# Keeping the gated results of four heads in SBUF and accumulating two projections in the seven-product stage's PSUM banks

## Chip, cores, metric

The kernel runs on 1 core of one Trainium2 chip. The metric is the device time of one launch in microseconds (us); the median of several runs counts.

## What is computed

A small transformer trunk of two layers over 512 frames, with 16 learned tokens in front (L = 528 positions, width 2048), batch 1, float32. Layer A is gated differential attention with 8 heads, layer B gated sliding-window attention with 32 query heads and 4 shared key/value heads. Cut to what matters here:

```
h = rms_norm(x, norm_g)
q, k, v, gate = split(h @ w_in, 4)              # layer A, w_in is 2048 x 8192
o = diff_attention(rope(q), rope(k), v, lam)    # 8 heads, head 7 last
o = rms_norm(o, subln_g) * (1 - lambda_init)
x = x + (o * silu(gate)) @ w_out                # layer A's output projection
k_sh, v_sh = split(rms_norm(x, kv_norm) @ w_kv) # the kv projection
...                                             # layer B, its projections, a final norm
```

## The kernel before

All data lie transposed, features on the 128 partitions and the 528 positions along the free dimension. Each product is made in three passes of a split arithmetic: an operand is cut into a high part (ScalarE copies it rounded, L96 or L739) and a low part (VectorE subtracts, L98, L100 or L740), and high x high, high x low, low x high are accumulated in PSUM. So each weight tile of 128 x 1024 costs one ScalarE and one VectorE instruction of about 1.1 us each before TensorE can use it; these are issued under `tc.high_priority()` (`wunit`, `form`).

Layer A's input projection (w_in) is worked in 32 pairs of 128-row tiles, `PAIRS[0]` to `PAIRS[31]`. The first three are multiplied plainly (`plain`), the other 29 by a scheme with seven products in place of eight (`product`, L361, in the order 1, 5, 2, 6, 3, 4, 7), each of 24 matmuls with 264 columns. The products accumulate in the PSUM pool psP, in the bank tiles B (two buffers), C and D (one each); `BANK` says which product uses which. ScalarE or VectorE empties each bank after its product. Pairs 0 to 23 give q, k and v of the 8 heads, which go to DRAM (`qkv_dram`); pairs 24 to 31 give the gates of heads 0 to 7. A head's attention (`heads_attend`) runs in small steps between the matmuls of later pairs; the result of head h goes to `o_dram[h]`, that of head 7 last, during pair 27.

`finish_gate` works up a gate: it has the head's two 128 x 528 result rows loaded (`gate_in`, L714, on GpSimd's DMA queue) into buffers of the pool ld, which has two; forms the silu in three steps (L725, L727, L728); multiplies by the loaded row on GpSimd (L729); and writes the product to `og_dram` (L731). `og_load` (L742, GpSimd's queue) reads such rows back into the five rows of po5, and `og_in` (L746) splits them into high and low parts for the output projection. The rows of head 7 alone are split from the ld buffer. In the last pairs these steps are spread as the loop at L792 says: rows 0 to 3 are loaded in pair 28 and split in pair 29, the others loaded from pair 30 on and split in pair 31. The high and low parts lie in quads, places of 128 x 2112 words handed out by `Quads`; the forms of product i give theirs back (`Q.free(*ft[i])`) after the last use.

Behind pair 31 the pools of layer A are closed and a new PSUM pool psA with two buffers of two banks is opened (L824). `proj` (L135) multiplies one 128-row output tile: two weight halves, 96 matmuls of 264 columns, both column halves in one accumulator. The output projection has 16 such tiles, each emptied by one VectorE instruction over 528 columns (L871); the kv projection has four (L906 to L913). The output projection needs the first rows' parts at its start and those of the last four rows only in the last quarter of its depth. Then new pools serve layer B.

At the start, `norm_a` computes the norm of x (`rstd`) between the plain pairs, then transposes it to a column `rcol` (L266 to L274). The two results of a plain pair are emptied by ScalarE (L424) into e0x or e0y and into e1, which is one buffer; `finish_qk` scales them and writes them to `qkv_dram` (L480, GpSimd's queue), after which the buffer is free.

Instructions are put in order per engine by a planner that goes by priority and its own estimate of durations; every engine and every DMA queue then works through its list in that order.

Of the kernel before, what the change touches and what calls it, by code (L numbers as in the profile page):

```python
# [43 lines left out]
def trunk(tc, xT, w, vecs, sinks, rope, ident_in, out):  # L44
# [11 lines left out]
    psP = pa.enter_context(tc.tile_pool(name="psP", bufs=1, space=bass.MemoryType.PSUM))  # L56
    steps = deque()
# [77 lines left out]
    def proj(m, hi, lo, cols):  # L135
        acc = psA.tile([128, len(cols), 512], F32, tag="acc", name="acc")
        for half in range(2):
            whi, wlo = wunit(m, half)
            for part in (((whi, hi), (whi, lo)), ((wlo, hi),)):
                for k8 in range(8):  # L140
                    kt = half * 8 + k8
                    ws = slice(k8 * 128, k8 * 128 + 128)
                    for a, b in part:
                        for s, (c0, n) in enumerate(cols):
                            pe.matmul(  # L145
                                acc[:, s, 0:n], lhsT=a[:, ws], rhs=b[kt // 4][:, kt % 4, c0 : c0 + n],
                                start=(kt == 0 and a is whi and b is hi), stop=(kt == KT - 1 and a is wlo),
                            )
                    if kt % 4 == (1 if len(part) == 2 else 3):
                        tick(0.25)  # L150
        return acc
# [109 lines left out]
    def norm_a():  # L261
# [3 lines left out]
        tables(0, 1.0, 128, etmp("rr", "ropec"), ld.tile([128, L], F32, tag="ld", name="ropes"))  # L265
        t = psT.tile([128, 512], F32, tag="T", name="Tr")  # L266
# [130 lines left out]
    def plain(p, between):  # L397

        o = {}
        for t, half in ((0, 0), (1, 0), (0, 1), (1, 1)) if p.m == 0 else ((0, 0), (0, 1), (1, 0), (1, 1)):  # L400
# [17 lines left out]
            if t == 0:  # L418
                p.results()
            else:  # L420
                between()
                p.e[1] = etmp("e1", "e1")
# [291 lines left out]
    def gate_in(p, j, i):  # L714
        p.o.append(ld.tile([128, L], F32, tag="ld", name="ldo"))
        pl.dma_start(p.o[i], o_dram[j][i])

    def finish_gate(p, j, i):
# [10 lines left out]
        pl.tensor_tensor(out=o, in0=z, in1=o, op=ALU.mult)  # L729
        if j < 7:  # L730
            pl.dma_start(og_dram[j][i], o)  # L731
        else:
            split_og(14 + i, o)

    ogh, ogl, ogt = [], [], []

    def split_og(m, src):
        a, b = ogh[m // 4][:, m % 4, :], ogl[m // 4][:, m % 4, :]
# [3 lines left out]
    def og_load(*ms):  # L742
        for m in ms:
            pl.dma_start(po5[:, m % 5, :], og_dram[m // 2][m % 2])

    def og_in(q4):  # L746
# [4 lines left out]
        for m in range(4 * q4, min(4 * q4 + 4, 14)):  # L751
            split_og(m, po5[:, m % 5, :])
# [21 lines left out]
    for j in range(PLAIN):  # L774
# [7 lines left out]
        else:  # L782
            finish(j, 0)
            finish(j, 1)
    for _ in building:
# [6 lines left out]
    for j in range(PLAIN, 32):  # L792
        p, q = PAIRS[j], PAIRS[j + 1] if j < 31 else None
        for i in ORDER:
# [8 lines left out]
            elif i == 6 and j == 28:  # L803
                og_load(0, 1, 2, 3)
            elif i == 6 and j == 29:
                og_in(0)
            elif i == 6 and j == 30:
                og_load(4, 5, 6, 7, 8)
            if q:
                q.load(*{6: ("a",), 5: ("s1",), 7: ("s3",), 3: ("b",), 4: ("d",)}.get(i, ()))  # L810
            else:
                Q.free(*ft[i])
                if i == 1:
                    og_in(1)
                    og_load(9, 10, 11, 12)
                elif i == 5:
                    og_in(2)
                    og_load(13)
                elif i == 2:
                    og_in(3)  # L820
    drain()
    pA.close()
    pa.close()
    psA = psum("psA", 2)  # L824
# [38 lines left out]
    for m in range(KT):  # L863
# [6 lines left out]
        acc = proj(T_OUT_A + m, ogh, ogl, FULL)[:, :, 0:HALF]  # L870
        dve.tensor_tensor(out=two(xr), in0=acc, in1=two(xr), op=ALU.add)  # L871
# [22 lines left out]
    for i in range(4):  # L894
        acc = proj(T_KV + i, kh, kl, FULL)[:, :, 0:HALF]
# [9 lines left out]
        if i < 2:  # L905
            dve.tensor_tensor(out=two(t), in0=acc, in1=two(CR), op=ALU.mult)  # L906
            r = tmp("kr")
            dve.stream_shuffle(out=two(r), in_=acc, mask=swap)
# [3 lines left out]
        else:  # L912
            dve.tensor_tensor(out=two(t), in0=acc, in1=two(rstd), op=ALU.mult)  # L913
            for a, b, c in PIECES:
                act.activation(vx[i - 2][:, a:b], t[:, c : c + b - a], AF.Copy)
    X.free(*ktags)
    ps.close()
# [321 lines left out]
```

## Time and profile before

| | us |
|---|---|
| median of 3 runs (lowest to highest) | 1716.14 (1713.49 to 1717.56) |
| the profiled execution | 1715.63 |
| its span in the trace | 1713.9 |
| TensorE busy (PE) | 96% of the span |
| VectorE (DVE) | 66% |
| ScalarE (ACT) | 50% |
| GpSimd (POOL) | 12% |

In the rows below, times count from the start of the span. PE is a matmul, PEld a weight load, SP the engine that issues most loads; L12 is line 12 of the kernel. A name as `po<-og_dram` is output from input. "[7.68 <-DMA og_dram<-ldo]" says that the engine sat idle for 7.68 us before the instruction, until that DMA had landed. In a chain of waits each piece released the next. PEclk is TensorE's granted clock as a share of full speed.

### The profile page before, as it was taken

To read this page: it belongs to the slowest core of one execution; us is meant where nothing else is said; L and a number is where in the kernel's file an instruction comes from. 1 tells how busy PE (TensorE), PEld (TensorE's weight loads), DVE (VectorE), ACT (ScalarE), POOL (GpSimd) and SP (SyncE) were. 2 spreads that over 40 slices of the span, in tenths; PEclk is the share of its full clock that TensorE was granted. 3 is DMA by queue.
4 is the path that set the end of the run, shared out by engine and by line. 5 is a ranking of instruction groups with operands and counts; after the bars stand their busy time and mean duration, and the time that the engine had idled before them with its cause. 6 is when DMAs were issued, how large, how long until landed. Compare 5 with 4: busy or idle time off the path is not lost.

```text
span 1713.9 us, 28699 instructions
## 1 busy us (share of the span) xinstructions
PE 1651.7 (96%) x11383; PEld 1533.0 (89%) x11383; DVE 1130.0 (66%) x1710; ACT 862.3 (50%) x1628; POOL 212.2 (12%) x246
## 2 busy tenths in 40 slices
PE   8899999999999999889899999999999999999996
PEld 8899999999999999889899999888878888888886
DVE  7877869687687878668433347567766776762234
ACT  9556656566665656544323234254545554543331
POOL 0011111111111113333101110000000000000111
PEclk9999999999999999989899999999999999999998
DMA  8366767676677676677444454222212122233332
GB/s 270 125 180 187 202 168 209 188 212 180 182 220 188 202 213 183 213 197 224 152 137 140 134 152 157 99 83 78 73 63 74 62 81 68 74 117 123 123 117 98
DMA packets 83493, 254.81 MB, mean 149 GB/s; under 512 B 10400, under 2 KB 14624, under 8 KB 83360
## 3 DMA queue, kind: packets, MB, share of 16 engines
q1 hardware_dynamic: 47616, 161.25, 28.2%
q0 software_dynamic: 16992, 59.62, 15.1%
q10 hardware_dynamic: 18752, 32.12, 6.0%
q8 instruction: 89, 1.46, 0.3%
q14 instruction: 44, 0.36, 0.1%
HBM read 223.34 MB, written 29.61 MB: 148 GB/s over the span
## 4 chain that ended last, share of the span: by engine, by line
PE 79%; DVE 7%; issue 5%; DMA 4%; ACT 3%; POOL 2%; DVEq 0%; ACTq 0%; POOLq 0%; SPq 0%
PE acc L145 42%; PE B L355 9%; PE C L355 7%; PE D L355 7%; DVE wlo L98 2%; PE TB L200 1%; PE poB L1032 1%; PE acct L1151 1%; PE B L409 1%; PE po L634 1%; DMA qkv_dram<-e 1%; PE SB L984 1%; PE SB L983 1%; DMA po<-og_dram 1%; PE S L516 1%
## 5 line engine op out<-in xcount | busy, mean ns | idle before, releaser
L98 DVE TENSOR_TENSOR wlo<-raw,whi 128x1024 fp32r<-128x1024 f32 x140 | 171.9, 1228 | 240.5 <-PE acc L145 192.8
L96 ACT ACTIVATE whi<-raw 128x1024 fp32r<-128x1024 f32 x140 | 148.2, 1060 | 219.2 <-PE acc L145 191.3
L145 PE MATMUL acc<-hh,whi 128*128 128x512 f32 x512 | 202.9, 396 | 0.0
L145 PE MATMUL acc<-hl,whi 128*128 128x512 f32 x512 | 201.2, 393 | 0.0
L145 PE MATMUL acc<-hh,wlo 128*128 128x512 f32 x512 | 129.5, 393 | 0.0
L145 PEld LDWEIGHTS acc<-hh,whi 128*128 128x128 f32 x512 | 96.5, 189 | 21.2
L145 PEld LDWEIGHTS acc<-hh,wlo 128*128 128x128 f32 x512 | 95.9, 188 | 21.7
L145 PEld LDWEIGHTS acc<-hl,whi 128*128 128x128 f32 x512 | 96.6, 189 | 20.5
L98 DVE TENSOR_TENSOR wlo<-rs,whi 128x1024 fp32r<-128x1024 f32 x58 | 73.1, 1261 | 29.0 <-ACT whi L96 10.4
L96 ACT ACTIVATE whi<-ra 128x1024 fp32r<-128x1024 f32 x58 | 61.3, 1058 | 59.1 <-PE B L355 24.8
L248 POOL TENSOR_TENSOR ss<-ss,sq 128x528 f32<-128x528 f32 (+1 forms) x26 | 35.0, 1348 | 451.5 <-ACT sq L247 451.5
L96 ACT ACTIVATE whi<-rs 128x1024 fp32r<-128x1024 f32 x58 | 61.2, 1055 | 58.8 <-DMA qkv_dram<-e 20.8
L995 ACT ACTIVATE p<-SB,nm 128x208 f32<-128x208 f32 (+2 forms) x128 | 51.2, 411 | 68.3 <-DVE es L992 61.0
L96 ACT ACTIVATE whi<-rb 128x1024 fp32r<-128x1024 f32 x58 | 61.3, 1057 | 47.6 <-DVE rb L336 13.9
L327 POOL DMA_DIRECT2D rs<-in_w x58 | 51.8, 893 | 251.9 <-DMA rs<-in_w 87.3
L98 DVE TENSOR_TENSOR wlo<-rb,whi 128x1024 fp32r<-128x1024 f32 x58 | 72.4, 1249 | 14.8 <-PE D L355 7.1
L355 PE MATMUL B<-f7h,whi 128*128 128x264 f32 x232 | 60.3, 293 | 6.2 <-ACT e L380 6.2
L355 PE MATMUL D<-f4h,whi 128*128 128x264 f32 x232 | 60.0, 292 | 5.7 <-DVE e L370 3.2
L934 POOL TENSOR_TENSOR qr<-qr,SR 128x512 f32<-128x512 f32 x16 | 22.2, 1387 | 333.6 <-DVE qr L933 266.3
L355 PE MATMUL C<-f5h,whi 128*128 128x264 f32 x232 | 60.1, 292 | 0.0
L355 PE MATMUL C<-f5l,whi 128*128 128x264 f32 x232 | 59.6, 290 | 0.0
L355 PE MATMUL D<-f4l,whi 128*128 128x264 f32 x232 | 59.4, 289 | 0.0
(476 smaller groups left out, 5096.4 us busy)
## 6 DMA issues: line engine op xcount, KB each, us to landing
raw<-in_w SPq DMA_DIRECT2D x148, 512.0 KB, 3.3
rs<-in_w SPq DMA_DIRECT2D x58, 512.0 KB, 3.9
rs<-in_w POOLq DMA_DIRECT2D x58, 512.0 KB, 6.0
rd<-in_w SPq DMA_DIRECT2D x29, 512.0 KB, 4.3
ra<-in_w SPq DMA_DIRECT2D x29, 512.0 KB, 4.6
rb<-in_w SPq DMA_DIRECT2D x29, 512.0 KB, 4.9
qkv_dram<-e POOLq DMA_DIRECT2D x48, 264.0 KB, 4.5
hr<-h_dram ACTq DMA_DIRECT2D x32, 256.0 KB, 3.3
```

The costliest lines, as they stand in the source:

```text
L96: act.activation(hi, raw, AF.Copy, scale=sign)
L98: dve.tensor_tensor(out=lo, in0=raw, in1=f(hi), op=ALU.subtract)
L145: pe.matmul(acc[:, s, 0:n], lhsT=a[:, ws], rhs=b[kt // 4][:, kt % 4, c0 : c0 + n], start=(kt == 0 and a is whi and b is hi), stop=(kt == K ...
L200: pe.transpose(o, i, ident[0 : i.shape[0], 0 : i.shape[0]])
L248: self.engine.tensor_tensor(out=self.acc[i], in0=self.acc[i], in1=t, op=ALU.add)
L327: pl.dma_start(t, w[self.m + 1, 1 if n == "s1" else 0], accum_op=ALU.add)
L355: pe.matmul(o, lhsT=a[:, ws], rhs=b[:, k, :], start=(first and k == 0 and b is fh[i] and a is hi), stop=(last and k == 7 and a is lo), ski ...
L409: pe.matmul(o[t][s], lhsT=a[:, ws], rhs=b[:, k8, :], start=(half == 0 and k8 == 0 and a is x[0] and b is fh[i]), stop=(half == 1 and k8 == ...
L516: pe.matmul(o, lhsT=qh[:, m, qs], rhs=qh[:, 2 + m, ks], start=True, stop=False)
L634: pe.matmul(pov[:, dt, c0:256], lhsT=v_, rhs=w_[:, j, c0:256], start=(j == 0 and k == 0), stop=False)
L934: pl.tensor_tensor(out=r, in0=r, in1=SR[:, META:], op=ALU.mult)
L995: act.activation(p[:, rt, 0:W], Sv[:, rt, :], AF.Exp, bias=nm[:, rt : rt + 1], accum_out=s[:, rt : rt + 1])
```

## The change

Six things are edited.

- The accumulators of the output and kv projections are no longer tiles of a pool psA, but pairs of the bank tiles of psP, by turns (C, D) and (B, B); psP is closed behind the kv projection. Each half of 264 columns is emptied by an instruction of its own.
- For heads 4 to 7, `gate_in` loads the attention result into a place of its own in SBUF (`ograw`), three quads taken after pair 27 and po5; the gated product stays there and is split from there. For heads 0 to 3 it goes to DRAM as before, and all eight rows are read back in pair 29.
- The product with the gate is made on VectorE in place of GpSimd.
- All four groups of rows are split in pair 31, after its products 1, 5, 2 and 6; the split places are those products' freed quads.
- In plain pair 1, the second result goes to an ld buffer in place of e1.
- The transposes that give `rcol` are moved from `norm_a` behind the plain pairs (`rstd_column`).

```diff
     def proj(m, hi, lo, cols):
-        acc = psA.tile([128, len(cols), 512], F32, tag="acc", name="acc")
+        if psA is None:
+            acc = [bank(t) for t in ("CD", "BB")[turns[0] % 2]]
+            turns[0] += 1
+        else:
+            acc = psA.tile([128, len(cols), 512], F32, tag="acc", name="acc")
...
-                                acc[:, s, 0:n], lhsT=a[:, ws], rhs=b[kt // 4][:, kt % 4, c0 : c0 + n],
+                                acc[s] if psA is None else acc[:, s, 0:n], lhsT=a[:, ws], rhs=b[kt // 4][:, kt % 4, c0 : c0 + n],
...
         tables(0, 1.0, 128, etmp("rr", "ropec"), ld.tile([128, L], F32, tag="ld", name="ropes"))
+
+    def rstd_column():
+
         t = psT.tile([128, 512], F32, tag="T", name="Tr")
...
-                p.e[1] = etmp("e1", "e1")
+                p.e[1] = ld.tile([128, L], F32, tag="ld", name="e1") if p.m == 2 else etmp("e1", "e1")
...
     def gate_in(p, j, i):
-        p.o.append(ld.tile([128, L], F32, tag="ld", name="ldo"))
+        p.o.append(ld.tile([128, L], F32, tag="ld", name="ldo") if j < 4 else ograw[j // 2][:, 2 * (j % 2) + i, :])
         pl.dma_start(p.o[i], o_dram[j][i])
...
-        pl.tensor_tensor(out=o, in0=z, in1=o, op=ALU.mult)
-        if j < 7:
+        dve.tensor_tensor(out=o, in0=z, in1=o, op=ALU.mult)
+        if j < 4:
             pl.dma_start(og_dram[j][i], o)
-        else:
-            split_og(14 + i, o)
+        elif j == 7:
+            split_og(14 + i)
...
-    def og_load(*ms):
-        for m in ms:
-            pl.dma_start(po5[:, m % 5, :], og_dram[m // 2][m % 2])
+    def og_places():
+
+        ograw[0] = po5
+        for q4 in range(1, 4):
+            ograw[q4], t = Q.get([128, 4, L], F32, f"ograw{q4}")
+            ogrt.append(t)
+
+    def og_load():
+        for m in range(8):
+            pl.dma_start(ograw[m // 4][:, m % 4, :], og_dram[m // 2][m % 2])
...
+    rstd_column()
     for _ in building:
...
             if i == 7 and j == 27:
                 drain()
-            elif i == 6 and j == 28:
-                og_load(0, 1, 2, 3)
+                og_places()
             elif i == 6 and j == 29:
-                og_in(0)
-            elif i == 6 and j == 30:
-                og_load(4, 5, 6, 7, 8)
+                og_load()
...
                 Q.free(*ft[i])
-                if i == 1:
-                    og_in(1)
-                    og_load(9, 10, 11, 12)
-                elif i == 5:
-                    og_in(2)
-                    og_load(13)
-                elif i == 2:
-                    og_in(3)
+                if i in (1, 5, 2, 6):
+                    og_in((1, 5, 2, 6).index(i))
+    Q.free(*ogrt)
     drain()
     pA.close()
-    pa.close()
-    psA = psum("psA", 2)
+    psA = None
...
-        acc = proj(T_OUT_A + m, ogh, ogl, FULL)[:, :, 0:HALF]
-        dve.tensor_tensor(out=two(xr), in0=acc, in1=two(xr), op=ALU.add)
+        acc = proj(T_OUT_A + m, ogh, ogl, FULL)
+        for c, a in zip(T, acc):
+            dve.tensor_tensor(out=xr[:, c], in0=a, in1=xr[:, c], op=ALU.add)
...
-            dve.tensor_tensor(out=two(t), in0=acc, in1=two(CR), op=ALU.mult)
             r = tmp("kr")
-            dve.stream_shuffle(out=two(r), in_=acc, mask=swap)
+            for c, o in zip(T, acc):
+                dve.tensor_tensor(out=t[:, c], in0=o, in1=CR[:, c], op=ALU.mult)
+                dve.stream_shuffle(out=r[:, c], in_=o, mask=swap)
...
     X.free(*ktags)
+    pa.close()
     ps.close()
```

## Rows read from the trace of the kernel before

**Rows 1.** The page's first part: busy time, share of the span, instructions.
```profile
PE 1651.7 (96%) x11383; PEld 1533.0 (89%) x11383; DVE 1130.0 (66%) x1710; ACT 862.3 (50%) x1628; POOL 212.2 (12%) x246
```
**Rows 2.** What PE waited for: us in total, times, longest (whole span).
```profile
PE B L355 <- ACT e L380: 6.2, 1, 6.2
PE B L355 <- DVE wlo L100: 5.8, 4, 3.2
PE acc L145 <- DVE e L388: 5.7, 1, 5.7
PE B L409 <- ACT e L424: 5.6, 1, 5.6
...
PE D L355 <- DVE e L370: 3.2, 1, 3.2
```
**Rows 3.** Windows: pairs 27 to 31, two projection tiles; length, busy (instructions), PEclk, DMA.
```profile
698.50:722.50 24.00, 20.59 (x167) 20.20 (x166) 19.42 (x20) 11.60 (x16) 7.73 (x11) 1.00 0.76 227
722.50:754.70 32.20, 22.81 (x162) 22.39 (x161) 17.04 (x19) 12.13 (x18) 12.00 (x15) 0.87 0.66 198
754.70:774.70 20.00, 20.00 (x159) 20.00 (x158) 16.90 (x17) 9.83 (x15) 7.69 (x9) 0.95 0.76 215
774.70:795.20 20.50, 20.50 (x170) 20.50 (x169) 17.04 (x17) 9.28 (x13) 6.23 (x7) 1.00 0.75 204
795.20:830.70 35.50, 26.01 (x193) 25.43 (x191) 26.99 (x34) 16.48 (x24) 11.42 (x14) 0.87 0.67 205
830.70:844.50 13.80, 13.80 (x97) 13.80 (x98) 3.23 (x4) 3.41 (x4) 1.32 (x1) 0.84 0.32 113
844.50:856.20 11.70, 11.70 (x98) 11.70 (x98) 3.84 (x4) 3.40 (x4) 0.00 (x0) 1.00 0.43 137
```
**Rows 4.** Chain of waits in pair 28: start, us, what.
```profile
741.08 8.73 DMA po<-og_dram
...
750.39 1.04 ACT whi L96
...
751.76 8.28 PE B L355 x48
```
**Rows 5.** Timeline of POOL in pair 28: start, us, instruction, idle before.
```profile
749.67 0.54 POOL L716 DMA_DIRECT2D ldo<-o_dram  x1 [7.68 <-DMA og_dram<-ldo]
...
757.27 2.10 POOL L729 TENSOR_TENSOR ldo<-e,ldo 128x528 f32<-128x528 f32 x1
```
**Rows 6.** Timeline of PE: the stop in pair 2, the first projection matmul.
```profile
75.98 0.59 PE L409 MATMUL B<-f1h,whi 128*128 128x264 f32 x1 [5.57 <-ACT e L424]
...
830.69 0.78 PE L145 MATMUL acc<-og0h,whi 128*128 128x264 f32 x2 [5.75 <-DVE e L388]
```
**Rows 7.** Timeline of ACT near 76 us.
```profile
75.53 0.39 ACT L424 ACTIVATE e<-B 128x264 f32<-128x264 f32 x1 [4.62 <-DMA qkv_dram<-e]
...
79.33 0.39 ACT L424 ACTIVATE e<-C 128x264 f32<-128x264 f32 x1 [3.13 <-DMA qkv_dram<-e]
```
**Rows 8.** Window behind the stop in pair 2, columns as in rows 3.
```profile
76.00:82.00 6.00, 6.00 (x31) 6.00 (x32) 0.81 (x2) 1.02 (x4) 1.09 (x3) 0.60 0.91 314
```
**Rows 9.** Timeline of DVE: pair 28, and the first projection tile's eviction.
```profile
756.34 0.71 DVE L728 SCALAR_TENSOR_TENSOR e<-th,e 128x528 f32<-128x528 f32 x1 [0.26 <-ACT th L727]
...
758.10 2.35 DVE L98 TENSOR_TENSOR wlo<-rs,whi 128x1024 fp32r<-128x1024 f32 x1
...
845.83 0.70 DVE L871 TENSOR_TENSOR xr<-acc,xr 128x528 f32<-128x528 f32 x1
```
**Rows 10.** DVE groups by line, 795 to 835 us: busy us, mean ns, idle before.
```profile
L740 DVE TENSOR_TENSOR og2l<-po,og2h 128x528 fp32r<-128x528 f32 x4 | 2.8, 705 | 4.7 <-ACT og2h L739 4.7
...
L98 DVE TENSOR_TENSOR wlo<-rs,whi 128x1024 fp32r<-128x1024 f32 x2 | 2.4, 1219 | 0.0
...
L388 DVE TENSOR_TENSOR e<-B,e 128x264 f32<-128x264 f32 x2 | 0.8, 425 | 0.0
```
**Rows 11.** Timeline of DVE near 68 us.
```profile
68.01 0.71 DVE L189 SCALAR_TENSOR_TENSOR rstd<-va,rstd 128x528 f32<-128x528 f32 x1
```

More of the change, by code (lines that the diff above doesn't have):

```diff
@@ L56, in trunk @@
     psP = pa.enter_context(tc.tile_pool(name="psP", bufs=1, space=bass.MemoryType.PSUM))
+    turns = [0]
     steps = deque()
@@ L728, in finish_gate, with split_og @@
         dve.scalar_tensor_tensor(out=z, in0=th, scalar=1.0, in1=z, op0=ALU.add, op1=ALU.mult)
-        pl.tensor_tensor(out=o, in0=z, in1=o, op=ALU.mult)
-        if j < 7:
+        dve.tensor_tensor(out=o, in0=z, in1=o, op=ALU.mult)
+        if j < 4:
             pl.dma_start(og_dram[j][i], o)
-        else:
-            split_og(14 + i, o)
+        elif j == 7:
+            split_og(14 + i)
     ogh, ogl, ogt = [], [], []
-    def split_og(m, src):
-        a, b = ogh[m // 4][:, m % 4, :], ogl[m // 4][:, m % 4, :]
+    ograw, ogrt = {}, []
+    def split_og(m):
+        a, b, src = ogh[m // 4][:, m % 4, :], ogl[m // 4][:, m % 4, :], ograw[m // 4][:, m % 4, :]
         act.activation(a, src, AF.Copy)
         dve.tensor_tensor(out=b, in0=src, in1=f(a), op=ALU.subtract)
-    def og_load(*ms):
-        for m in ms:
-            pl.dma_start(po5[:, m % 5, :], og_dram[m // 2][m % 2])
+    def og_places():
[6 more added lines that the diff above has]
+            pl.dma_start(ograw[m // 4][:, m % 4, :], og_dram[m // 2][m % 2])
     def og_in(q4):
@@ L751, in og_in @@
         for m in range(4 * q4, min(4 * q4 + 4, 14)):
-            split_og(m, po5[:, m % 5, :])
+            split_og(m)
     def finish(j, i):
@@ L894, in trunk @@
     for i in range(4):
-        acc = proj(T_KV + i, kh, kl, FULL)[:, :, 0:HALF]
+        acc = proj(T_KV + i, kh, kl, FULL)
         a, ta = Y.get([128, 4, L], F32R, f"hh{i}")
@@ L912, in trunk @@
         else:
-            dve.tensor_tensor(out=two(t), in0=acc, in1=two(rstd), op=ALU.mult)
+            for c, o in zip(T, acc):
+                dve.tensor_tensor(out=t[:, c], in0=o, in1=rstd[:, c], op=ALU.mult)
             for a, b, c in PIECES:
```

## The prediction

> **What bounds the kernel now.** I read the profile from the coarse to the fine. The page first: TensorE (PE) is busy for 1651.7 of 1713.9 us [rows 1], so only what leaves PE idle, or lets its clock fall, can be won. Then the list of what PE waited for [rows 2]: four single waits of 5.7, 5.6, 6.2 and 3.2 us and a group of four that holds another of 3.2 us. The longest stand at the end of layer A and none repeats with the loop, so the list is a map of a few places. Third, the windows cut at the starts of the seven-product pairs 27 to 31 and of the first two output projection tiles [rows 3]. An undisturbed pair takes 20.0 to 20.5 us (pairs 29 and 30; I use 20.3), an undisturbed projection tile 11.7 us. Pair 27 takes 24.0, pair 28 takes 32.2, pair 31 with the handover 35.5, and the first projection tile 13.8. The excess is 3.7, 11.9, 15.2 and 2.1 us. The granted clock falls to 0.87 in the two long stretches, so part of the excess is matmuls at the lower of the two levels (1.2 GHz in place of 2.4), not idling: after the 6.2 us wait, 48 matmuls take 8.28 us [rows 4], where 170 in 20.5 us [rows 3] would put them at 5.8.
>
> Why does PE stop there? The chain of waits through pair 28 [rows 4] runs backwards from PE to a bank eviction and a weight split on ScalarE (ACT), and from these to a DMA that reads gated rows back from DRAM (po<-og_dram, 8.73 us from issue to landing). ACT works in order: the split of a gated row (L739) that waits for this load holds up the weight split and the eviction behind it, which PE needs. The load in turn stands in GpSimd's (POOL's) queue behind gate_in's load of the next head (L716), and this waits 7.68 us for the write of an earlier gated row [rows 5], because the two ld buffers hold rows until they are written out. So it is a round trip: product on POOL, write, buffer free, next load, read back, split. Pair 31 ends in the same loop: the D bank's reader (L370) and the last B bank's reader (L388) make the waits of 3.2 and 5.7 us [rows 2].
>
> The other place is the start. PE stops for 5.57 us before the second tile of pair 2 [rows 6], for a bank that ACT empties only at 75.53, since its target, the single e1 buffer, is still being written to DRAM [rows 7]. From 76 to 82 the clock is 0.60: 31 matmuls in 6 us [rows 8], where 170 per 20.5 us would be 50; that is 19 x 0.12 = 2.3 us more.
>
> **The change, part by part.**
>
> *Round trip removed.* For heads 4 to 7 the attention result is loaded into a place of its own, multiplied there and split from there. Six writes and six loads go, and no load waits for a write any more. The first four heads still go through DRAM, but their eight loads are issued in pair 29 and first used in pair 31, some 25 us later, against the 8.73 us to landing of the one in the chain [rows 4]. Pair 28 then falls to 20.3: **-11.9 us**, bounds 0 (if ACT still finds a row missing) and -11.9. The eight loads stand in POOL's queue ahead of the adds onto weight tiles; at 0.54 us of issue each [rows 5] these are held for 4.3 us, beside a pair of 20.3 us in which such an add is used once. I count 0; if the cover is gone it is up to 4.3 us, once.
>
> *Product from POOL to VectorE (DVE).* Sixteen products of about 0.71 us (the gate's neighbour L728 of the same shape [rows 9]) come onto DVE: 1.4 us a pair. Against that, a weight split that ran beside POOL's product (2.10 us [rows 5]) took 2.35 us [rows 9], where the groups give a mean of 1.22 [rows 10]: about 1.1 us comes back for each overlap. Pairs 28 to 30 have DVE busy for 17 us of their 20 or more [rows 3], so both hide: 0. Pair 27 is where the last head's normalisation loads DVE (19.42 of 24.0 us [rows 3]); I leave its 3.7 us excess as it is, bounds -3.7 and +1.4.
>
> *All splits in pair 31.* Here the change adds a load on a loaded engine. Today DVE is busy 27.0 us in the 35.5 of pair 31 [rows 3], with 9 to 10 row splits in it; the new one has 14 splits and about three products there. With splits at 0.705 [rows 10] and products at 0.71: 27.0 - 9 x 0.7 + 14 x 0.7 + 3 x 0.7 = 32.6 us; one or two overlaps with POOL's product, 1.1 us each as above, go, so 31. PE wants 20.3 for the pair, and the last rows are needed only some 7.8 us into the first projection tile (its last quarter of depth, two thirds of 11.7). That leaves 31 - 28.1 = 2.9 us; I take **3 us** that PE still loses, of the 15.2 + 2.1 that go: **-14.3 us**. The upper end: DVE does every split before PE may enter the projection, 31 - 20.3 = 10.7 us and a clock dip of 2.1, so -4.5. The lower end: nothing is lost, -17.3. What is late next after L388 is L370 of product 3, which reads bank C, queued on DVE behind splits. I take the value near the lower end because weight splits are issued at high priority and pass the row splits, and the need is staggered over the tile.
>
> *Bank tiles.* The first projection tile takes C and D, whose last readers belong to products 3 and 4, instead of a new pool that waits for all readers of the old one; that is what lets the 5.7 us wait go (in the sum above). Each of 20 tiles is emptied by two instructions of 264 columns at 0.425 in place of one of 528 at 0.70 [rows 9, 10]: 0.15 x 20 = 3 us of DVE in all, beside 11.7 us tiles in which DVE is busy 3.84 [rows 3]: 0. In the kv tiles a shuffle is halved in the same way: 0. The old banks are now given up behind the kv stage; the next stage's accumulators are new tiles whichever way, so 0, bounds 0 and +2 (a bank's eviction).
>
> The Trainium skill speaks against this edit: by "TensorE: Matmul & The Clock Gate", section "A second HAM failure mode: psum-queue depth-cycling", cycling accumulators through PSUM banks leaves TensorE small idles between groups of matmuls often enough for its clock to fall back over and over. By that rule the twenty tiles would lose clock; pairs 29 and 30, which cycle these same banks, run at 0.95 and 1.00 [rows 3], so the trace does not bear it out here, and the sum stands without it.
>
> *The start.* The second result of pair 1 goes into an ld buffer. The norm's scratch holds these until L189 ends at 68.7 [rows 11]; PE needs the bank at 70.4 (75.98 less 5.57 [rows 6]), and the eviction itself takes 0.39 [rows 7]. So it can be in time, by 1.3 us, if ACT's order puts it first; one weight split of about 1 us ahead of it [rows 4] makes it about 1 us late. Of 5.57 + 2.3 = 7.9 us I take **-6 us**, bounds -7.9 and 0. The five transposes and the two small copies behind them only move past the plain pairs, still on PE and DVE: 0. What is late next: pair 2's first result, which waits until 79.33 for the write of pair 0's [rows 7], and the reloads of head 0 behind it in ACT's queue. PE would be at pair 3 11.7 us after 70.4 (a tile of the same 96 matmuls [rows 3]), near 82.1; an ACT that keeps today's order may not be ready for it there.
>
> Sum against the profiled execution (span 1713.9, 1715.6 in all): 11.9 + 14.3 + 6 = 32.2, so 1683.4; the median of the runs shown, 1716.14, is 0.5 above that execution, so **1684**.
>
> **The rivals.**
>
> 1. *VectorE becomes the bound of pair 31.* For it: 31 us of work against 20.3. Against: the weight splits go first and most rows are needed late. Then the handover gives 4.5 in place of 14.3: 1684 + 9.8 = **1694**.
> 2. *The start's wait only moves.* For it: ACT waits in order for a write of pair 0's at 79.33 [rows 7] whatever PE does, and for the reloads of head 0 that follow such writes. Against: the bank in question no longer depends on them. The 6 us go: **1690**.
> 3. *The round trip is still there*, the change not doing what it says: the loads of the first four heads and of heads 4 to 7 share POOL's queue with the adds onto weights, and an ACT split still waits for one. For it: order on the queues is a planner's. Against: each load has a place of its own and some 25 us. Then half of 11.9 + 14.3 goes: 1684 + 13.1 = **1697**.
> 4. *The other side: projection tiles wait for their banks.* If a tile's banks are not free when it starts, PE stands until both halves are read. Today the eviction of the first tile (L871) starts at 845.83 and ends at 846.53 [rows 9], 2.0 us after that tile's end at 844.5 [rows 3]. Such a wait on 19 tiles is 38 us: **1722**, slower. It decides from the point at which an eviction lags one tile (11.7 us), since two pairs of banks take turns; now it lags 2.0, and DVE is a third busy. The Trainium skill's page "TensorE: Matmul & The Clock Gate", in the section named above, describes a loss of this kind.
>
> **How the numbers follow.** Forecast 0.48; rival 1 0.20; rival 2 0.15; rival 3 0.08; rival 4 0.06; nothing to be seen, by gains and losses that cancel, 0.03. 0.2% of the time is 3.4 us, about what a measurement of this kernel can tell from no change. Faster is forecast and rivals 1 to 3, 0.91; same 0.03; slower 0.06. The range runs from 1677 (no loss in pair 31, 3, pair 27's 3.7 half won, 2, and the start's full 7.9, 2) to 1698, which takes in rivals 1 to 3 one at a time. Rivals 1 and 2 together, 1700, and rival 4 are left out.
>
> **What would show it.** Right: pair 28 at 20 to 21 us with clock 1.00; no ACT wait on po<-og_dram; no PE wait on e L424 above 1.5 us and no low clock near 76 us; first projection matmul near 803 to 806 where it is 830.69 now [rows 6] (start 6 and pair 28 12 earlier, pair 31 itself 6 to 9 shorter), with the rest of the loss inside the first tile. From the second tile on, each stretch as long as before. Wrong: ACT or DVE waiting for a gated row in pair 28, a PE wait on DVE of 5 us or more near the handover (rival 1), PE waits near 80 to 90 us (rival 2), or waits before each projection tile (rival 4).

## The result, and the profile after

The kernel after takes 1675.62 us (median of 4 runs, 1672.12 to 1678.31), the kernel before 1715.63 (4 runs): a ratio of 0.9766, 95% interval 0.9744 to 0.9788. The profiled execution of after takes 1676.46 us with a span of 1674.7, against 1715.63 and 1713.9. So 39.2 us of span went where 32.2 were forecast. 1684 was too high, and the result lies 1.4 us below the range (1677 to 1698).

First the page of after (as rows 1), then the head of its list of what PE waited for (as rows 2), and one later line:

```profile
PE 1640.9 (98%) x11383; PEld 1523.9 (91%) x11383; DVE 1129.5 (67%) x1750; ACT 863.4 (52%) x1628; POOL 180.4 (11%) x218
```
```profile
PE C L417 <- ACT wu L97: 3.8, 1, 3.8
PE TB L205 <- DVE p L1014: 3.6, 3, 2.1
PE lps L462 <- DVE subg L467: 3.0, 1, 3.0
PE B L363 <- DVE wlo L101: 2.8, 3, 1.0
PE Tv L205 <- DMA ldv<-qkv_dram: 2.6, 1, 2.6
...
PE B L363 <- ACT e L432: 0.5, 1, 0.5
```

None of the long waits of [rows 2] is left, and asked for 660 to 830 us alone (pair 26 to the third projection tile) the list has no line. Line numbers have moved: product L363, projection matmul L150, the gate's product L737, row splits L748 and L749, eviction L880.

The windows of after, as rows 3, are pairs 27, 28 and 31 and two stretches as long as the first two projection tiles:

```profile
691.30:711.80 20.50, 20.50 (x171) 20.50 (x170) 19.51 (x22) 12.53 (x16) 6.67 (x11) 1.00 0.80 243
711.80:732.30 20.50, 20.50 (x171) 20.50 (x170) 15.77 (x20) 9.12 (x14) 5.81 (x10) 1.00 1.01 318
773.30:794.03 20.73, 20.73 (x169) 20.56 (x169) 20.70 (x30) 16.41 (x27) 0.86 (x1) 1.00 0.52 142
794.03:805.70 11.67, 11.61 (x96) 11.40 (x95) 9.60 (x14) 3.83 (x6) 0.00 (x0) 1.00 0.48 159
805.70:817.40 11.70, 11.70 (x99) 11.70 (x98) 3.90 (x5) 4.03 (x5) 0.00 (x0) 1.00 0.43 137
```

PE is busy throughout, at clock 1.00. VectorE (the DVE column, fourth after the length) is busy 20.70 of 20.73 us in pair 31 and 9.60 of 11.67 behind it, and PE loses next to nothing to it.

Where the time went, cut at the first matmul of each stage in the timeline of PE (the planner interleaves products of neighbouring pairs, so the cuts differ from those of [rows 3] by up to 2.7 us; the sums do not suffer):

| stage | before | after | won | forecast |
|---|---|---|---|---|
| start, to pair 3 | 90.4 | 81.9 | 8.5 | 6 |
| pairs 3 to 26 | 608.0 | 609.4 | -1.4 | 0 |
| pair 27 | 24.4 | 20.5 | 3.9 | 0 |
| pair 28 | 34.1 | 20.5 | 13.6 | 11.9 |
| pairs 29 and 30 | 41.0 | 41.0 | 0 | 0 |
| pair 31 and handover | 32.8 | 20.8 | 12.0 | 14.3, with the next row |
| first two projection tiles | 25.4 | 23.7 | 1.7 | |
| the rest | | | 0.8 | 0 |

But for rounding that is the 39.2 us.

The start in after (PE, then ACT, then the window of rows 8):

```profile
81.89 0.39 PE L363 MATMUL B<-f1h,whi 128*128 128x264 f32 x1 [0.48 <-ACT e L432]
```
```profile
68.46 0.67 ACT L432 ACTIVATE e<-B 128x264 f32<-128x264 f32 x2 [5.98 <-DVE rstd L194]
```
```profile
76.00:82.00 6.00, 5.52 (x46) 5.24 (x46) 3.98 (x4) 2.17 (x5) 0.89 (x2) 1.00 0.79 270
```

The eviction that came at 75.53 [rows 7] now comes at 68.46, the moment the norm's scratch is free. The clock from 76 to 82 is 1.00 where it was 0.60 [rows 8], and pair 3 waits 0.48 us.

### The profile page after: what moved, and what is told of

It reads as the page before. It is cut to its first block, busy times and chain, and to the rows that moved or that the text cites. A ratio compares the mean times of both kernels' runs of the same rounds, so it can differ in the third digit from the quotient of the medians.

```text
span 1674.7 us, 28671 instructions
## 1 busy us (share of the span) xinstructions
PE 1640.9 (98%) x11383; PEld 1523.9 (91%) x11383; DVE 1129.5 (67%) x1750; ACT 863.4 (52%) x1628; POOL 180.4 (11%) x218
## 4 chain that ended last, share of the span: by engine, by line
PE 88%; DVE 5%; DMA 3%; ACT 2%; issue 1%; POOL 1%; ACTq 0%; DVEq 0%; SPq 0%; POOLq 0%
PE acc L150 29%; PE B L363 12%; PE D L363 9%; PE C L363 9%; PE B L150 7%; PE C L150 3%; PE D L150 3%; PE B L417 2%; PE TB L205 1%; PE poB L1044 1%; PE acct L1163 1%; PE po L642 1%; DVE wlo L99 1%; PE C L417 1%; DMA qkv_dram<-e 1%
## 5 line engine op out<-in xcount | busy, mean ns | idle before, releaser
L99 DVE TENSOR_TENSOR wlo<-raw,whi 128x1024 fp32r<-128x1024 f32 x140 | 171.7, 1227 | 169.1 <-PE acc L150 89.2
L150 PE MATMUL acc<-hh,whi 128*128 128x512 f32 x512 | 203.1, 397 | 0.0
L150 PE MATMUL acc<-hl,whi 128*128 128x512 f32 x512 | 201.3, 393 | 0.0
L150 PE MATMUL acc<-hh,wlo 128*128 128x512 f32 x512 | 129.4, 393 | 0.0
L150 PEld LDWEIGHTS acc<-hh,wlo 128*128 128x128 f32 x512 | 96.0, 188 | 21.8
L150 PEld LDWEIGHTS acc<-hh,whi 128*128 128x128 f32 x512 | 96.5, 189 | 21.1
L150 PEld LDWEIGHTS acc<-hl,whi 128*128 128x128 f32 x512 | 96.7, 189 | 20.5
L99 DVE TENSOR_TENSOR wlo<-rs,whi 128x1024 fp32r<-128x1024 f32 x58 | 70.7, 1219 | 18.9 <-ACT po L650 5.7
L99 DVE TENSOR_TENSOR wlo<-rb,whi 128x1024 fp32r<-128x1024 f32 x58 | 70.8, 1220 | 15.3 <-PE D L363 8.8
L363 PE MATMUL D<-f2h,whi 128*128 128x264 f32 x232 | 59.5, 290 | 0.0
L363 PE MATMUL D<-f2l,whi 128*128 128x264 f32 x232 | 59.4, 290 | 0.0
L363 PE MATMUL B<-f7h,whi 128*128 128x264 f32 x232 | 58.8, 288 | 0.0
L363 PE MATMUL C<-f5h,whi 128*128 128x264 f32 x232 | 58.8, 287 | 0.0
L363 PE MATMUL B<-f1h,whi 128*128 128x264 f32 x232 | 58.1, 285 | 0.5 <-ACT e L432 0.5
L363 PE MATMUL D<-f4h,whi 128*128 128x264 f32 x232 | 58.5, 287 | 0.0
```

The costliest lines, as they stand in the source:

```text
L99: dve.tensor_tensor(out=lo, in0=raw, in1=f(hi), op=ALU.subtract)
L150: pe.matmul(acc[s] if psA is None else acc[:, s, 0:n], lhsT=a[:, ws], rhs=b[kt // 4][:, kt % 4, c0 : c0 + n], start=(kt == 0 and a is whi ...
L363: pe.matmul(o, lhsT=a[:, ws], rhs=b[:, k, :], start=(first and k == 0 and b is fh[i] and a is hi), stop=(last and k == 7 and a is lo), ski ...
```

## The experiments

All ratios are against runs of the kernel before that were taken together with the kernel's own on the same chip, with 95% intervals. The medians of the kernel before lie between 1715.6 and 1719.5 us, 0.2% apart, so I compare ratios, and places by the stages of each trace. A ratio of 0.001 is 1.7 us.

| kernel | us | ratio | 27 | 28 | 29 | 31 | two tiles |
|---|---|---|---|---|---|---|---|
| before | | 1 | 24.4 | 34.1 | 20.5 | 32.8 | 25.4 |
| rows_alone | 1706.37 | 0.9931 (0.9907 to 0.9954) | 20.6 | 28.1 | 27.3 | 27.0 | 24.9 |
| product_alone | 1713.80 | 0.9964 (0.9944 to 0.9984) | 25.4 | 27.9 | 22.1 | 34.5 | 24.9 |
| rows_and_product | 1693.29 | 0.9859 (0.9844 to 0.9874) | 20.5 | 25.1 | 20.5 | 24.6 | 24.9 |
| banks_alone | 1714.43 | 0.9970 (0.9952 to 0.9988) | 27.0 | 35.0 | 20.7 | 26.5 | 26.4 |
| start_alone | 1707.26 | 0.9939 (0.9919 to 0.9960) | 25.5 | 32.4 | 20.8 | 34.5 | 25.6 |
| buffer_alone | 1711.65 | 0.9963 (0.9944 to 0.9981) | 26.2 | 32.3 | 20.5 | 32.8 | 25.1 |
| after | 1675.62 | 0.9766 (0.9744 to 0.9788) | 20.5 | 20.5 | 20.5 | 20.8 | 23.7 |
| after_product_on_gpsimd | 1693.01 | 0.9860 (0.9841 to 0.9880) | 20.6 | 27.7 | 29.6 | 22.7 | 25.5 |
| after_own_pool | 1683.10 | 0.9809 (0.9783 to 0.9836) | 20.5 | 20.5 | 20.5 | 24.6 | 25.8 |
| after_column_in_place | 1682.92 | 0.9796 (0.9771 to 0.9822) | 21.8 | 20.5 | 20.5 | 22.9 | 23.9 |
| after_vector_load | 1684.16 | 0.9806 (0.9791 to 0.9821) | 20.5 | 20.5 | 20.5 | 28.0 | 23.6 |
| after_vector_load_four | 1683.75 | 0.9802 (0.9781 to 0.9823) | 20.5 | 23.5 | 20.5 | 23.9 | 23.9 |
| after_one_bank_pair | 1701.90 | 0.9903 (0.9882 to 0.9925) | 20.5 | 20.5 | 20.5 | 20.8 | 26.0 |

(Pairs and tiles in us, from each profiled execution.)

### Parts of the change, put into the kernel before

**rows_alone**: the rows of heads 4 to 7 are kept and all splits are in pair 31. The product stays on GpSimd, and accumulators and start are as before.

```diff
-        p.o.append(ld.tile([128, L], F32, tag="ld", name="ldo"))
+        p.o.append(ld.tile([128, L], F32, tag="ld", name="ldo") if j < 4 else ograw[j // 2][:, 2 * (j % 2) + i, :])
...
-        if j < 7:
+        if j < 4:
             pl.dma_start(og_dram[j][i], o)
```

> The kernel before with the rows of heads 4 to 7 kept on chip and all splits in pair 31, but the product on GpSimd, the projections in their own pool and the start as before. Theory R (the stop in pair 27 is part of the round trip, through ScalarE waiting for read-back rows just before it): pairs 27 and 28 both fall to 20.5 us, the handover keeps a wait for all readers of the old pool; 17.5 us less from the two pairs and some 5 to 9 from pair 31, 1690 to 1693. Theory C (the stop in pair 27 comes from GpSimd's product slowing VectorE, or from the last head's normalisation as predicted): pair 27 stays near 24, pair 28 falls; 1693 to 1697.

Measured 0.9931: 12 us, where the forecast had put 26.2 on the round trip and the handover. Pair 27 came down to 20.6, but pairs 28 and 29 still lose 7.6 and 6.8 us: together they take 55.3 us, where before took 54.6. GpSimd's queue shows why. First pair 28 (POOL, ACT and PE of rows_alone, with the idle time and its releaser in brackets):

```profile
715.75 1.16 POOL L704 DMA_DIRECT2D o_dram<-po  x2
725.10 0.54 POOL L753 DMA_DIRECT2D po<-og_dram  x1 [8.19 <-DMA o_dram<-po]
725.65 1.08 POOL L716 DMA_DIRECT2D ograw<-o_dram  x2
726.74 1.32 POOL L729 TENSOR_TENSOR ldo<-e,ldo 128x528 f32<-128x528 f32 x1
```
```profile
728.08 0.39 ACT L385 ACTIVATE e<-D 128x264 f32<-128x264 f32 x1 [5.81 <-POOL ldo L729]
728.37 1.05 ACT L96 ACTIVATE whi<-rb 128x1024 fp32r<-128x1024 f32 x1
```
```profile
729.47 0.59 PE L355 MATMUL D<-f2h,whi 128*128 128x264 f32 x1 [2.90 <-ACT whi L96]
```

Read it from the bottom. PE waits for a weight split. That split stands behind an eviction in ACT's order, and the eviction waits 5.81 us for the buffer e, which the gate's product (L729) is the last to read. The product itself stands in POOL's queue behind the issue of a read-back (L753) that waits 8.19 us for a write, that of an attention result out of the place po, which the read-back fills. The rows of heads 4 to 7 no longer go round, but products queue behind those that do.

In pair 29 the PE wait comes by another way (POOL, ACT, and PE's wait from its list):

```profile
745.72 0.55 POOL L753 DMA_DIRECT2D ograw<-og_dram  x1 [9.07 <-DMA og_dram<-ldo]
746.44 0.89 POOL L327 DMA_DIRECT2D rs<-in_w  x1 [0.17 <-ACT whi L96]
```
```profile
754.37 1.06 ACT L96 ACTIVATE whi<-rs 128x1024 fp32r<-128x1024 f32 x1 [7.92 <-DMA rs<-in_w]
```
```profile
PE C L355 <- ACT whi L96: 3.8, 1, 3.8
```

Here a read-back waits 9.07 us for the write of a gated row. What stands behind it is no product but a DMA that adds onto a weight tile (L327); ACT waits 7.92 us for it, and PE 3.8 us for ACT's split. The product has a part in this too, since the write can only be issued behind it; how much of the loss is the product's and how much the add's was not tried apart.

**product_alone**: only the product moves to VectorE.

```diff
-        pl.tensor_tensor(out=o, in0=z, in1=o, op=ALU.mult)
+        dve.tensor_tensor(out=o, in0=z, in1=o, op=ALU.mult)
```

> The kernel before with the product of result and gate on VectorE in place of GpSimd alone. Theory C: pair 27 falls from 24.4 to about 21, 3 to 4 us less, 1712. Theory R: pair 27 stays near 24; the round trip gets shorter by about 1 us per row, so 0 to 4 us less from pair 28 and 31. As predicted: 0.

Measured 0.9964, 6 us: pair 28 falls by 6, pair 31 grows by 1.7, and pair 27 stays at 25.4. So pair 27's excess is not GpSimd's product running beside VectorE. Just ahead of this pair, which begins at 700.1 here, ACT waits for rows that are read back, and in its order nothing behind them can go on (product_alone, ACT). The chain of waits runs on from the second of these rows, through a weight split and an eviction on ACT, to VectorE's weight splits in pair 27:

```profile
692.72 0.65 ACT L739 ACTIVATE og0h<-po 128x528 fp32r<-128x528 f32 x1 [5.69 <-DMA po<-og_dram]
...
700.02 0.65 ACT L739 ACTIVATE og0h<-po 128x528 fp32r<-128x528 f32 x1 [1.94 <-DMA po<-og_dram]
```

In rows_alone, where ACT splits no row before pair 31, pair 27 takes 20.6. What the waits for the rows cost and what the splits themselves cost there was not tried apart.

**rows_and_product**: both edits, in the kernel before.

> The kernel before with the rows of heads 4 to 7 kept on chip and the product on VectorE, but the projections in their own pool and the start as before. Theory Q (in the run with the rows alone the products stood in GpSimd's queue behind DMA issues that waited for other DMAs, and held the buffers that ScalarE empties banks into): pairs 27 to 30 all at 20.5 us, 17.5 us less than before for these four; the handover keeps 3 to 6 us of its wait for the old pool; about 1690 in all, some 16 less than with the rows alone. As predicted (the product's move is worth 0): pairs 28 and 29 stay near 28 and 27 us, as with the rows alone, 1706.

Measured 0.9859, so the product is worth 12 us more once the rows stay, where alone it was worth 6 (and 1.3 by the spans of the two profiled executions). Its list of PE's waits from 660 to 840 us has two lines:

```profile
PE acc L145 <- DVE e L388: 3.7, 1, 3.7
PE C L355 <- DVE wlo L98: 3.0, 1, 3.0
```

**banks_alone**: only the projections' accumulators become bank tiles of psP.

> The kernel before with the projections in the bank tiles of the seven-product stage alone. If the handover wait comes from the new pool waiting for all readers: 5 to 8 us less (the wait of 5.7 and its clock dip), 1708 to 1711. If it comes from the last rows, which are late through the round trip: the wait moves behind the first matmuls, 0 to 3 us less. If alternating banks cost TensorE: stretches of more than 11.7 us per tile and 30 us or more slower.

Measured 0.9970, 5 us. Pair 31 with the handover falls by 6.3, but pairs 25 and 27, on which the edit has no work, take 3.3 and 2.6 us longer, and the two tiles 1.0: the same instructions stand in another order. This alone does not price the bank tiles, so they were taken out of after, below.

**start_alone** and **buffer_alone**: the ld buffer for pair 1's second result with the moved transposes, and without them.

```diff
-                p.e[1] = etmp("e1", "e1")
+                p.e[1] = ld.tile([128, L], F32, tag="ld", name="e1") if p.m == 2 else etmp("e1", "e1")
```

> The kernel before with the two start edits alone (ld buffer for the second result of pair 1, transposes behind the plain pairs). If the start's gain is a removed wait with its clock dip and is independent of the rest: 8.5 us less, 1707; pair 3 starts near 82 in place of 90.4 and every later stretch is as before. As predicted: 6 us less, 1710. If the wait only moves: no change, 1716.

> The kernel before, with the second result of plain pair 1 in an ld buffer and nothing else. Theory: pair 3 starts at 82 to 83 instead of 90.4, and as with both edits of the start 1 to 4 us of it are given back in pairs 27 and 31, so 1707 to 1711 (kernel before about 1716). Rival: without the moved transposes the stop only moves to them, and pair 3 starts at 85 or later.

Pair 3 starts at 81.4 with both and at 84.0 with the buffer alone, against 90.4: the buffer is worth 6.4 us there, the moved transposes 2.6. The ratios are 0.9939 and 0.9963, 10 and 6 us, so little of the gain is lost later. What PE waits for in buffer_alone before pair 3 is the eviction that rival 2 spoke of, 1.56 us of it:

```profile
84.00 0.39 PE L355 MATMUL B<-f1h,whi 128*128 128x264 f32 x1 [1.56 <-ACT e L424]
```

### Parts taken out of the kernel after

**after_product_on_gpsimd**: the product back on GpSimd.

> The changed kernel with the product put back on GpSimd. Theory Q: pairs 28 and 29 go back to 26 to 28 us and pair 31 to 22 to 27; 13 to 20 us slower than the changed kernel, 1689 to 1696. As predicted: no change, 1676. Theory C (GpSimd's product slows VectorE): a loss of 1 us per overlap, spread over pairs 24 to 31, 2 to 8 us.

Measured 0.9860: 16 us are lost again, 7.2 in pair 28 and 9.1 in pair 29. Waits of this kernel from 690 to 800 us show both chains of rows_alone, first that of pair 28, then that of pair 29:

```profile
POOL po L760 <- DMA o_dram<-po: 9.2, 1, 9.2
ACT e L393 <- POOL ldo L737: 7.1, 1, 7.1
PE D L363 <- ACT whi L97: 3.1, 1, 3.1
```
```profile
POOL ograw L760 <- DMA og_dram<-ldo: 15.0, 2, 8.6
ACT whi L97 <- DMA rs<-in_w: 21.4, 3, 8.7
PE C L363 <- ACT whi L97: 4.2, 1, 4.2
```

**after_own_pool**: the accumulators back in psA.

> The kernel after, with the accumulators of both projections back in a pool of their own (psA), emptied in one instruction over 528 columns. What are the bank tiles worth once the splits are in pair 31? Theory: they are the handover. With the pool, the first projection tile waits for every reader of the old banks, as in rows and product together, where pair 31 with its handover took 24.6 us and the first tile 13.3: here the same, so some 4 us in pair 31 and up to 4 in the first tiles are lost, and the time is 1682 to 1686 (kernel after 1675.6). Rival: VectorE keeps up in pair 31 either way, and the bank tiles are worth nothing: 1676, pair 31 at 21 us.

Measured 0.9809, 7 us slower than after (the two intervals just touch); in the trace pair 31 takes 3.8 us more and the first two tiles 2.1. PE's first projection matmul, here and in after, with the first matmul into C and the first of the second tile (B) in after:

```profile
796.04 0.78 PE L145 MATMUL acc<-og0h,whi 128*128 128x264 f32 x2 [3.69 <-DVE e L390]
```
```profile
794.03 0.28 PE L150 MATMUL D<-og0h,whi 128*128 128x264 f32 x1
...
796.59 0.28 PE L150 MATMUL C<-og0h,whi 128*128 128x264 f32 x1
...
803.29 0.40 PE L150 MATMUL B<-og0h,whi 128*128 128x264 f32 x2
...
806.05 0.28 PE L150 MATMUL C<-og3h,wlo 128*128 128x264 f32 x1
```

and VectorE in after at the same place:

```profile
795.98 0.44 DVE L378 TENSOR_TENSOR e<-C,e 128x264 f32<-128x264 f32 x1
...
797.28 0.44 DVE L396 TENSOR_TENSOR e<-B,e 128x264 f32<-128x264 f32 x1
...
803.98 0.71 DVE L749 TENSOR_TENSOR og3l<-ograw,og3h 128x528 fp32r<-128x528 f32 x1 [0.71 <-ACT og3h L748]
```

With a pool of its own the first tile cannot start before L390 (the reader of the last B bank) is done. With bank tiles it starts in D alone, 1.95 us before VectorE even begins to empty C. It moves on to C once that is read. The second tile, in B, begins at 803.29, while half of the matmuls of the first's last quarter (og3h, og3l) are still to come: VectorE finishes the last row at 804.69.

**after_column_in_place**: the transposes back between the plain pairs.

> The kernel after, with the five transposes of the norm's column back between the plain pairs. It splits the start's 8.5 us between the ld buffer and the moved transposes. Theory: the ld buffer frees the bank and is nearly all of it; pair 3 starts within 1 us of 81.9, the time is 1675 to 1678. Rival: the transposes, for which PE waits on the norm's row and its copies, hold PE up once the bank no longer does, and they are the 2.5 us by which the start won more than forecast: pair 3 at 84 to 85, the time 1678 to 1680.

Measured 0.9796, 5 us slower, though its interval overlaps that of after. Pair 3 starts at 83.4, 1.5 us later; pairs 27 and 31 take 1.3 and 2.1 us more, for which the edit itself has no work there. Neither theory's figure was right: the transposes are 1.5 of the start's 8.5 us by this trace and 2.6 by the pair of runs above, and the rest is another order of the planner.

**after_one_bank_pair**: all projection tiles in C and D.

```diff
-            acc = [bank(t) for t in ("CD", "BB")[turns[0] % 2]]
+            acc = [bank(t) for t in ("CD", "CD")[turns[0] % 2]]
```

> The changed kernel with every projection tile in the banks C and D, none in the two B banks: each tile must wait until both halves of the one before are read. Rival 4's price: 2.0 us per tile on 19 tiles, 38 us, 1714. If the wait is only for the first half (C is read first and needed first): 1.2 us per tile, 23 us, 1699. If the granted clock also falls at each wait: 60 us or more.

Measured 0.9903, 23 us slower than after (28.7 by the spans of the two profiled executions). Its waits on an eviction, then the longer of those in the kv stage:

```profile
PE C L150 <- DVE kr L918: 8.1, 2, 6.1
PE C L150 <- DVE xr L880: 7.9, 16, 0.5
```
```profile
1017.25 0.59 PE L150 MATMUL C<-kh,whi 128*128 128x264 f32 x1 [6.08 <-DVE kr L918]
```

In the output projection a wait without the second pair of banks is 0.5 us at most: PE goes on in C as soon as L880 has read that half. A tile then takes 12.4 us in place of 11.7. In the kv projection it reaches 6.08: VectorE is at the norm and its tables before it can empty the first tile. Two windows of 13 us, each a little longer than an output tile, and that of the kv wait:

```profile
820.00:833.00 13.00, 12.50 (x103) 12.32 (x102) 3.90 (x5) 3.39 (x4) 0.00 (x0) 1.00 0.38 113
833.00:846.00 13.00, 12.50 (x103) 12.32 (x102) 3.90 (x5) 3.40 (x4) 1.37 (x1) 1.00 0.44 142
...
1013.00:1026.00 13.00, 8.75 (x52) 8.75 (x53) 10.24 (x23) 4.85 (x7) 0.00 (x0) 0.74 0.38 121
```

The clock stays at 1.00 with a 0.5 us stop in every tile, and is 0.74 in the stretch with the 6.08 us stop. Cut as in the stage table, 12.9 us of the loss lie between the first output and the first kv matmul and 11.0 between this and the attention of layer B; another 4.6 lie in pairs 3 to 23, where this edit has no work.

**after_vector_load** and **after_vector_load_four**: the row subtractions L749 are made twice, all fourteen or the first four; some 9.1 and 2.6 us more work on VectorE in pair 31. The diff is that of the fourteen; for the four the condition is `q4 == 0`.

```diff
             split_og(m)
+            if True:
+                dve.tensor_tensor(out=ogl[q4][:, m % 4, :], in0=ograw[q4][:, m % 4, :], in1=f(ogh[q4][:, m % 4, :]), op=ALU.subtract)
```

> The changed kernel with each of the 14 row subtractions of pair 31 made twice (the second writes the same values): 14 x 0.65 = 9.1 us more on VectorE in pair 31 and the handover, where it is busy 20.7 of 20.7 us. If VectorE is on the edge there (rival 1 of the prediction begins just behind it): TensorE loses 8 to 11 us, 1684 to 1687. If the need is staggered so that VectorE has slack: 0 to 3 us.

> The kernel after, with the four row subtractions of the first group made twice on VectorE: 2.6 us more of it in pair 31, early in the pair. Where does VectorE's edge lie? With fourteen made twice, 9.1 us of added work cost 8.5. Theory: there is no slack at all, the added work is lost nearly one to one: 1677.5 to 1678.5. Rival: the edge lies 1 to 3 us behind the present load, and an early load is caught up over the pair: 1675.5 to 1676.

Fourteen: 0.9806, 7 us slower than after. Pair 31 is 7.2 us longer, at a clock of 0.88 over its 28 us, with a single new wait, for the reader of bank D:

```profile
PE D L363 <- DVE e L378: 5.2, 1, 5.2
```

Four: 0.9802, 6 us slower and more than either theory gave, though its interval overlaps that of after. In the trace pair 31 is 3.1 us longer for 2.6 us of early work, so little or no slack is left (after_column_in_place shows that order alone can move this pair by 2.1). The other 3.0 us are in pair 28, where nothing was added. There VectorE and GpSimd (after_vector_load_four) show:

```profile
726.09 0.71 DVE L737 TENSOR_TENSOR ldo<-e,ldo 128x528 f32<-128x528 f32 x1 [5.58 <-DMA ldo<-o_dram]
726.72 1.22 DVE L99 TENSOR_TENSOR wlo<-rb,whi 128x1024 fp32r<-128x1024 f32 x1
```
```profile
721.15 0.56 POOL L724 DMA_DIRECT2D ldo<-o_dram  x1 [5.60 <-DMA og_dram<-ldo]
```

and the same two places in after:

```profile
723.15 0.71 DVE L737 TENSOR_TENSOR ldo<-e,ldo 128x528 f32<-128x528 f32 x1 [2.83 <-DMA ldo<-o_dram]
```
```profile
718.22 0.56 POOL L724 DMA_DIRECT2D ldo<-o_dram  x1 [2.86 <-DMA og_dram<-ldo]
```

The round trip of heads 0 to 3 is still there. Its last load waits for a write, and the product that needs the row now holds VectorE, with weight splits queued behind it. In after the wait is 2.83 us and PE does not feel it. Here it is 5.58 and PE stands 2.7 us for the weight split L99; in rows_and_product it is 5.71, and PE stands the 3.0 us listed above. So of pair 28's gain 3.0 to 4.6 us (it takes 23.5 and 25.1 there, 20.5 in after) rest on luck in the order.

## Why the prediction was right and wrong

The time came out 1.4 us below the range because two terms of the sum were too small: pair 27, put at 0, gave 3.9, and the start, put at 6, gave 8.5. The step that failed as a mechanism is another one. The prediction priced the product's move at 0 and said that, with the rows of heads 4 to 7 kept, "no load waits for a write any more". The runs show loads that wait 8.19 and 9.07 us in POOL's queue with these rows kept, the product and the weight adds standing behind them, and 12 us won when the product leaves that queue.

**What bounds.** Right: the gain came from the places named, the start and the pairs from 27 to the first projection tiles, and PE's clock there is now 1.00.

**Round trip, -11.9.** The size was right (pair 28 took 20.5), the attribution was not, so that the size fits is luck. Keeping the rows alone leaves pairs 28 and 29 with 14.4 us lost. Three things were wrong in the working. The eight loads do not come in pair 29: in rows_alone the planner spreads them from ahead of pair 27 (693.72) to 755.41, and in after the last is issued at 732.12, just before that pair begins, so that rows are still being written. And so loads still wait for writes, 8.19 and 9.07 us in rows_alone, and in after

```profile
732.12 0.54 POOL L760 DMA_DIRECT2D ograw<-og_dram  x1 [6.23 <-DMA og_dram<-ldo]
```

where it costs nothing: the add behind it, at 734.86, waits 2.21 us more for VectorE. Third, the adds onto weight tiles were priced at the issue time of the loads ahead of them, at most 4.3 us and counted as 0, not at the waits of these loads; PE stood 3.8 us for one in rows_alone. The row that I quoted for the loop before, 7.68 us at 749.67, is also a turn too late: the load in the chain was issued at 741.08, behind this one:

```profile
738.06 0.55 POOL L716 DMA_DIRECT2D ldo<-o_dram  x1 [5.57 <-DMA og_dram<-ldo]
```

**Product to VectorE, 0.** This is the step that failed as a mechanism. I weighed only what the product costs VectorE and what it does to a neighbour there. I did not ask what stands ahead of it on POOL: issues that wait for other DMAs. [rows 5] already showed one 7.68 us wait in that queue, and the product in it. Moving it off is worth 6 us alone, 12 with the rows kept and 16 out of the full change. In the total this error did not show, because its gain had been booked under the round trip.

Moving it also added a wait that I did not name, of the product for its row with VectorE's weight splits behind it. It costs nothing at 2.83 us (after) and 3.39 us (after_own_pool), and 2.7 to 3.0 us of standing at 5.58 (after_vector_load_four) and 5.71 (rows_and_product).

**Pair 27, left as it is.** Wrong by 3.9 us, the largest single miss in the sum. I put its excess down to the last head's normalisation because VectorE was busy 19.42 of 24.0 us [rows 3]. It is busy 19.51 in after as well, in 20.5 us. The excess went with the early splits, which rows_alone moves to pair 31: the planner runs the first of them, which the loop writes in pair 29, ahead of pair 27, and ACT waits there for their rows. Whether the waits or the work of the splits cost the time is open; VectorE is on the path too, for inside this pair of before ACT waits 7.17 us for it (rb, at 710.80). The stated bound of -3.7 nearly held it; the point I took did not.

**Splits in pair 31 and handover, -14.3.** Nearly right: 13.7 by the stage table, or 29.2 of excess in pairs 28 and 31 and the first tile, of which 27.3 went and 26.2 were forecast. Of the 3 us that PE was to lose, 0.6 is left (44.5 us for pair 31 and two tiles; 20.5 and twice 11.7 would be 43.9). VectorE's load was as computed (20.70 + 9.60 = 30.3 us, forecast 31), and the last quarter began 7.8 us into the tile, as reckoned. But PE did not need all of its rows then: the two tiles interleave, and the low part of the last row, done at 804.69, is first used 10.8 us into the tile:

```profile
804.83 0.30 PE L150 MATMUL C<-og3l,whi 128*128 128x264 f32 x1
```

The handover needs the bank tiles besides. With a pool of its own PE waits 3.69 us for the reader of the last B bank, pair 31 takes 3.8 us more, and the first two tiles 2.1 more, the first of them at a clock of 0.81.

**Bank tiles, 0 for themselves.** The evictions in halves cost nothing (tiles of 11.7 us as before). What they are worth in the handover is some 6 us by the trace, now measured.

**The start, -6.** The mechanism was right, the term too small: 8.5, beyond even its bound of 7.9. I let ACT's order cost 1 to 2 us, but the eviction went first, at 68.46. And the moved transposes, costed at 0, gave 1.5 to 2.6 of it.

**Pairs 3 to 26.** 1.4 us were lost in all; pair 25 alone lost 1.7 (28.1 before, 29.8 after). PE waits 2.6 us for a load (Tv<-ldv) in after. Before and banks_alone, which do the same work there, give 28.1 and 31.4, so the planner's order alone can move it that far; the cause was not pursued.

So the sum was off by 7.0 us of span, but for rounding: +3.9 from pair 27, +2.5 from the start, +1.1 from pairs 28 to 31 with the handover, +0.8 from the rest, -1.4 from pairs 3 to 26.

**The rivals.** Rival 1 (VectorE bounds pair 31) did not come, but begins just behind this load: 2.6 us of extra work cost 3.1. Rival 2 (the wait only moves) came to 0.5 us of its 6. Rival 3 (an ACT split still waits for a round trip) did not come in this form. In rows_alone the round trip did hold PE up, by way of POOL's queue, and its cousin on VectorE, above, did so in two of the experiments. Rival 4's place was right and its price too high: without a second pair of banks a tile waits 0.5 us and takes 0.8 longer, not 2.0, in the output projection, and one kv tile 6.1; with two pairs, nothing. Against the rule of the Trainium skill that the prediction weighed ("TensorE: Matmul & The Clock Gate", "A second HAM failure mode: psum-queue depth-cycling"), the trace shows clock 1.00 over the output tiles of after (794 to 981 us), and over those of after_one_bank_pair (798 to 998 us), which stop 0.5 us each.

**The range.** Its low end added half of pair 27 and 3 us of pair 31 to a full 7.9 of the start. Taking each stated bound (-3.7, -17.3, -7.9) in full, with the 11.9, would have reached 1675 (1715.6 - 40.8 = 1674.8). What the low end left out is the other half of pair 27, 1.9 us, and the start went 0.6 beyond its bound; the measured time lies 1.4 below.

## What to carry to other kernels

When an instruction is moved off an engine, price what stands ahead of it in the queue it leaves, not only its duration. A short operation behind DMA issues that wait for other DMAs can cost as much as their waits, if a buffer that it reads is needed by someone on the path; so can a load that is issued from the same queue. (Leaving the product there and issuing the read-backs from another queue is the other way out; it was not tried.) And when two neighbouring stalls share a stalled engine, follow the idle time of that engine (here ACT just ahead of pair 27, waiting for po<-og_dram) before putting one of them down to a busy neighbour.

## What was not expected of the hardware and the planner

A whole pair ran with VectorE busy 20.70 of 20.73 us and PE still at clock 1.00 without a stop. And edits in one stage shift other stages by 1 to 5 us through the planner's order: pair 25 took 28.1 us in before and 31.4 in banks_alone, with the same work. A single small part, put in or taken out by itself, is therefore priced by the stages it touches, not by the total.
